# Row softmax in 3 whole-row buffers instead of 6 half-row buffers, and the last three stores moved to SyncE's queue

## The chip, the cores and the metric

The kernel runs on one core of a Trainium2 chip. The metric is the device time of one execution in microseconds (us). Three executions of the kernel before took 2497.65, 2497.72 and 2498.47 us; their median is 2497.72 us. The core has compute engines that run their own instruction streams; this kernel uses VectorE (DVE), ScalarE (ACT) and SyncE (SP, which here only issues transfers). Transfers between the core's memory (SBUF, 128 partitions) and the chip's main memory are issued from SP's queue and from ACT's queue, and 16 DMA engines carry them out.

## The reference

The kernel computes a softmax with temperature over the last axis of a float32 tensor of 16 x 256 x 32768. The temperature is 1.0.

```python
def reference(logits, temperature):
    scaled = logits / temperature
    scaled = scaled - scaled.max(axis=-1, keepdims=True)
    exp_scaled = np.exp(scaled)
    return (exp_scaled / exp_scaled.sum(axis=-1, keepdims=True)).astype(np.float32)
```

The tensor has 4096 rows of 32768 elements, 536.87 MB. It is read once and written once, so 1073.74 MB have to pass the DMA engines.

## The kernel before

**Tiles.** Each row is cut into two halves of 16384 elements, and each half takes one partition, so a tile is 128 partitions (64 rows) by 16384 elements (64 KB per partition, 8.39 MB). There are G = 64 tiles. A tile has C = 2 chunks of `_CW` = 8192 elements (32 KB per partition, 4.19 MB). SBUF holds `_BUFS` = 6 chunk buffers, three tiles' worth; chunk i lives in buffer i % 6 and its result is written in place.

**Loads and stores.** `load(i)` (lines 103 to 118) runs on SP's queue. It first waits until the buffer's earlier store has landed (line 106), then issues one DMA of 4.19 MB (line 112); in the first and the last tile each chunk is loaded as two pieces of `_EDGE` = 4096 elements (2.1 MB). `store(i)` (lines 120 to 133) runs on ACT's queue: it waits until DVE has scaled the chunk and issues one DMA (line 128), or two in the last tile.

**Compute of one tile** (lines 137 to 230). For each chunk DVE waits for its load and takes the negated maximum (line 156); ACT replaces the chunk by exp(x - max) and accumulates the sum (line 170). When ACT has finished the tile's last chunk, DVE swaps maxima and sums between the two partitions of one row (line 183) and takes the row's maximum (line 187), ACT forms the correction factors (line 194), DVE the corrected sum (line 200) and its reciprocal (line 212). Then DVE scales each chunk in place (line 221). In the last tile all this is done in four pieces of 4096 instead of two of 8192.

**Order.** Every engine's order is written out by hand; nothing is reordered. Six chunk loads are issued first. Then, tile by tile, comes the compute, and after it for each of the tile's chunks its store and the load of the chunk that takes its buffer, six chunks on. SP therefore issues loads alone, in order, each when its buffer's store has landed; ACT issues a tile's stores between its own work on that tile and on the next. The waits are semaphore waits of the issuing engine, so everything behind a wait on that engine is held up too.

```python
    for i in range(_BUFS):
        load(i)
    for g in range(G):
        compute(g)
        for c in range(C):
            i = g * C + c
            store(i)
            j = i + _BUFS
            if j < n_chunks:
                load(j)
```

Of the kernel before, what the change touches and what calls it, by code (L numbers as in the profile page):

```python
# [6 lines left out]


_CW = 8192
_BUFS = 6  # L10
_EDGE = 4096


class Stream:
# [40 lines left out]
@with_exitstack  # L55
def kernel(
    ctx: ExitStack,
    tc: tile.TileContext,
    logits: bass.AP,
    temperature: bass.AP,  # L60
    out: bass.AP,
):
    nc = tc.nc
    inv_t = 1.0 / float(temperature)
    P = nc.NUM_PARTITIONS
    fp32 = mybir.dt.float32
# [7 lines left out]
    C = W // _CW  # L74
    assert W * 2 == V and C * _CW == W and (N * 2) % P == 0
    x = xf.rearrange("n (h v) -> (n h) v", h=2)
    o = of.rearrange("n (h v) -> (n h) v", h=2)
    G = N * 2 // P
    n_chunks = G * C
    swap = [i ^ 1 for i in range(32)]  # L80

    ctx.enter_context(tc.tile_critical())  # L82
    X = nc.alloc_sbuf_tensor("xs", [P, _BUFS * _CW], fp32)
    KM = 2 * C
    T = [nc.alloc_sbuf_tensor(f"t{q}", [P, 4 * KM], fp32) for q in range(2)]
    E = [nc.alloc_sbuf_tensor(f"ee{q}", [P, 2 * KM], fp32) for q in range(2)]
    J = [nc.alloc_sbuf_tensor(f"junk{q}", [P, 2 * KM], fp32) for q in range(2)]
    R = [nc.alloc_sbuf_tensor(f"row{q}", [P, 4], fp32) for q in range(2)]

    sp = Stream(nc, nc.sync, "sp")  # L90
    dve = Stream(nc, nc.vector, "dve")
    act = Stream(nc, nc.scalar, "act")
    loads = [[Landing(nc, f"ld{b}{h}") for h in range(_CW // _EDGE)] for b in range(_BUFS)]
    stores = [Landing(nc, f"st{b}") for b in range(_BUFS)]
    scaled = {}
    landed = {}
    fine = {}
    freed = {b: [] for b in range(_BUFS)}

    def spans(total, step):  # L100
        return [(s, min(step, total - s)) for s in range(0, total, step)]

    def load(i):
        g, c = divmod(i, C)
        b = i % _BUFS
        sp.wait(*freed[b])
        pieces = spans(_CW, _EDGE if g in (0, G - 1) else _CW)
        rows = slice(g * P, (g + 1) * P)
        for k, (s, n) in enumerate(pieces):
            lane = loads[b][k]  # L110
            lane.add(
                nc.sync.dma_start(  # L112
                    out=X[:, b * _CW + s : b * _CW + s + n],
                    in_=x[rows, c * _CW + s : c * _CW + s + n],
                )
            )
        landed[i] = [lane.token() for lane in loads[b] if lane.count]
        fine[i] = len(pieces) > 1

    def store(i):  # L120

        g, c = divmod(i, C)
        b = i % _BUFS
        rows = slice(g * P, (g + 1) * P)
        for s, n in spans(_CW, _EDGE if g == G - 1 else _CW):
            act.wait(scaled[i, s])
            stores[b].add(
                nc.scalar.dma_start(
                    out=o[rows, c * _CW + s : c * _CW + s + n],
                    in_=X[:, b * _CW + s : b * _CW + s + n],  # L130
                )
            )
        freed[b] = [stores[b].token()]

    hist = {}

    def compute(g):
        step = _EDGE if g == G - 1 else _CW
        per = _CW // step
        K = C * per  # L140
        t, e, j_, r = T[g % 2], E[g % 2], J[g % 2], R[g % 2]
        tv = t[:, 0 : 4 * K].rearrange("p (a b k) -> p a b k", a=2, b=2)
        old = hist.get(g - 2)
        sums = []
        for c in range(C):
            i = g * C + c
            b = i % _BUFS
            for s, n in spans(_CW, step):
                k = c * per + s // step
                xs = X[:, b * _CW + s : b * _CW + s + n]  # L150
                piece = s // _EDGE
                dve.wait(*(landed[i][piece : piece + 1] if fine[i] and step == _EDGE else landed[i]))
                if old:
                    dve.wait(old["ee"], old["tr"])
                m = dve.done(
                    nc.vector.tensor_reduce(  # L156
                        out=t[:, k : k + 1], in_=xs, axis=mybir.AxisListType.X, op=A.max, negate=True
                    )
                )
                if inv_t != 1.0:  # L160
                    dve.wait(m)
                    m = dve.done(
                        nc.vector.tensor_scalar_mul(
                            out=t[:, k : k + 1], in0=t[:, k : k + 1], scalar1=inv_t
                        )
                    )
                act.wait(m)
                sums.append(
                    act.done(
                        nc.scalar.activation(  # L170
                            out=xs,
                            in_=xs,
                            func=Exp,
                            bias=t[:, k : k + 1],
                            scale=inv_t,
                            accum_out=t[:, K + k : K + k + 1],
                        )
                    )
                )
# [31 lines left out]
        dve.wait(tr)  # L211
        rc = dve.done(nc.vector.reciprocal(out=r[:, 2:3], in_=r[:, 1:2]))  # L212
        dve.wait(rc)
        for c in range(C):
            i = g * C + c
            b = i % _BUFS
            for s, n in spans(_CW, step):
                k = c * per + s // step
                xs = X[:, b * _CW + s : b * _CW + s + n]
                scaled[i, s] = dve.done(  # L220
                    nc.vector.tensor_scalar(  # L221
                        out=xs,
                        in0=xs,
                        scalar1=e[:, k : k + 1],
                        scalar2=r[:, 2:3],
                        op0=A.mult,
                        op1=A.mult,
                    )
                )
        hist[g] = {"ee": ee, "tr": tr}  # L230

    for i in range(_BUFS):
        load(i)
    for g in range(G):
        compute(g)
        for c in range(C):
            i = g * C + c
# [40 lines left out]
```

## Time and profile before

| what | value |
|---|---|
| time of the profiled execution | 2497.72 us |
| its span | 2495.9 us |
| median of three executions | 2497.72 us |
| moved by DMA | 1073.84 MB, mean 430 GB/s over the span |
| DVE busy | 1723.7 us (69%), 644 instructions |
| ACT busy | 944.5 us (38%), 325 instructions |
| store DMAs (ACT's queue) | 126 of 4096 KB and 4 of 2048 KB |
| load DMAs (SP's queue) | 124 of 4096 KB and 8 of 2048 KB |

The span is the stretch that the profile covers; 1.8 us of the time lie around it. Busy time is time in which an engine executes; the DMA rate is given by the profile for 40 equal slices of the span and, when asked, for any stretch. A packet is what one DMA engine moves in one go: here one partition's contiguous piece, 32 KB of a whole chunk and 16 KB of an edge piece, besides a 4-byte one per DMA and engine that counts up the semaphore.

### The profile page before, as it was taken

The numbers are of one execution on the slowest core, as the hardware profiler recorded it, in microseconds if no ns is written. First come the engines' busy times: TensorE is split into PE (matmuls) and PEld (weight loads), VectorE is DVE, ScalarE is ACT, GpSimd is POOL, SyncE is SP. The second block draws the span as 40 slices with busy tenths as digits, with TensorE's granted clock in tenths as the row PEclk, the third lists the DMA queues.
The fourth block names the chain that finished last, engine by engine and source line by source line (L and its number), as shares of the span: only waits on it lengthen the run. The fifth ranks groups of instructions, "written<-read, shape, count | busy, mean of one in ns | idle before, by whom it ended". The sixth has DMA issues, their size and how long they took to land.

```text
span 2495.9 us, 1288 instructions
## 1 busy us (share of the span) xinstructions
DVE 1723.7 (69%) x644; ACT 944.5 (38%) x325; POOL 0.2 (0%) x4
## 2 busy tenths in 40 slices
DVE  6777766767667676676766767767667676676763
ACT  3344334343343433434334333343333433434332
POOL 0000000000000000000000000000000000000000
DMA  9999999999999999999999999999999999999997
GB/s 412 432 433 435 430 436 430 436 430 436 432 434 435 431 435 430 436 431 434 435 431 436 429 437 430 436 432 433 435 430 435 431 436 432 434 434 431 435 433 337
DMA packets 37738, 1073.84 MB, mean 430 GB/s; under 512 B 4192, under 2 KB 4192, under 8 KB 4192
## 3 DMA queue, kind: packets, MB, share of 16 engines
q1 hardware_dynamic: 19008, 536.88, 49.9%
q10 hardware_dynamic: 18720, 536.88, 49.8%
q14 instruction: 10, 0.08, 0.0%
HBM read 536.87 MB, written 536.87 MB: 430 GB/s over the span
## 4 chain that ended last, share of the span: by engine, by line
DMA 62%; another core or an unknown queue 15%; DVE 15%; ACT 7%; SPq 0%; issue 0%; DVEq 0%
DMA out_dram<-xs 38%; DMA xs<-in_logits_dram 23%; DVE t L156 9%; ACT xs L170 7%; DVE xs L221 5%; SPq L112 0%; ACT ee L194 0%; DVE row L212 0%; DVE row L187 0%; DVE t L183 0%; DVE junk L200 0%; DVE row L200 0%; SPq L273 0%; DVEq L31 0%
## 5 line engine op out<-in xcount | busy, mean ns | idle before, releaser
L170 ACT ACTIVATE xs<-xs,t 128x8192 f32<-128x8192 f32 (+1 forms) x130 | 912.1, 7016 | 1498.5 <-DVE t L156 1498.5
L156 DVE TENSOR_REDUCE t<-xs 128x1 f32<-128x8192 f32 (+1 forms) x130 | 1111.1, 8551 | 263.8 <-DMA xs<-in_logits_dram 263.8
L221 DVE TENSOR_SCALAR xs<-xs,ee,row 128x8192 f32<-128x8192 f32 (+1 forms) x130 | 576.6, 4478 | 2.3
L183 DVE LOAD_MASK_SELECT t<-t x64 | 0.9, 14 | 463.1 <-ACT xs L170 463.1
L194 ACT ACTIVATE ee<-t,row 128x4 f32<-128x4 f32 x64 | 19.0, 297 | 27.0 <-DVE row L187 27.0
L200 DVE CUSTOM_DVE_ANT_1 junk<-ee,t 128x4 f32<-128x4 f32 x64 | 10.4, 163 | 23.3 <-ACT ee L194 23.3
L170 ACT ACTIVATION_READ_ACCUMULATOR xs<-xs,t 128x1 f32 x130 | 24.2, 186 | 0.0
L212 DVE RECIPROCAL row<-row 128x1 f32<-128x1 f32 x64 | 10.5, 164 | 2.2
L187 DVE TENSOR_REDUCE row<-t 128x1 f32<-128x4 f32 x64 | 10.1, 157 | 2.2
L183 DVE STREAM_SHUFFLE t<-t 128x4 f32<-128x4 f32 x64 | 9.9, 155 | 0.0
L200 DVE DVE_READ_ACCUMULATOR2_ANT row<- 128x1 f32 x64 | 5.3, 82 | 0.0
L170 ACT ACT_TABLE_LOAD x1 | 1.3, 1283 | 0.9 <-SPq L82 0.9
L259 POOL MEMSET const-bfloat16-1.0<- 128x1 bf16 x1 | 0.1, 101 | 0.0
L259 POOL MEMSET const-uint8-127<- 128x1 uint8 x1 | 0.1, 101 | 0.0
L259 POOL MEMSET const-float32-0.0<- 128x1 f32 x1 | 0.1, 98 | 0.2 <-issue 0.2
L259 POOL MEMSET const-float32-1.0<- 128x1 f32 x1 | 0.1, 98 | 0.0
## 6 DMA issues: line engine op xcount, KB each, us to landing
out_dram<-xs ACTq DMA_DIRECT2D x126, 4096.0 KB, 49.4
xs<-in_logits_dram SPq DMA_DIRECT2D x124, 4096.0 KB, 26.6
xs<-in_logits_dram SPq DMA_DIRECT2D x8, 2048.0 KB, 21.2
out_dram<-xs ACTq DMA_DIRECT2D x4, 2048.0 KB, 10.2
```

The source lines that it names most:

```text
L156: nc.vector.tensor_reduce(out=t[:, k : k + 1], in_=xs, axis=mybir.AxisListType.X, op=A.max, negate=True)
L170: nc.scalar.activation(out=xs, in_=xs, func=Exp, bias=t[:, k : k + 1], scale=inv_t, accum_out=t[:, K + k : K + k + 1],)
L183: nc.vector.stream_shuffle(out=t[:, 2 * K : 4 * K], in_=t[:, 0 : 2 * K], mask=swap)
L187: nc.vector.tensor_reduce(out=r[:, 0:1], in_=tv[:, :, 0, :], axis=mybir.AxisListType.XY, op=A.min)
L194: nc.scalar.activation(out=ev, in_=tv[:, :, 0, :], func=Exp, bias=r[:, 0:1], scale=-1.0)
L200: nc.vector.tensor_tensor_reduce(out=j_[:, 0 : 2 * K].rearrange("p (a k) -> p a k", a=2), in0=ev, in1=tv[:, :, 1, :], scale=1.0, scalar=0. ...
L212: rc = dve.done(nc.vector.reciprocal(out=r[:, 2:3], in_=r[:, 1:2]))
L221: nc.vector.tensor_scalar(out=xs, in0=xs, scalar1=e[:, k : k + 1], scalar2=r[:, 2:3], op0=A.mult, op1=A.mult,)
L259: nc = _bacc.Bacc("TRN2", target_bir_lowering=False, num_devices=1)
```

## The change

The chunk disappears as the unit of transfer and of buffering. `_BUFS` becomes 3 buffers of a whole tile (64 KB per partition, the same SBUF bytes in all). A load is one DMA of 8.39 MB, still four pieces of 4096 elements in the first and the last tile; it waits for the landing of the store of the whole tile that was in the buffer. A store is one DMA of 8.39 MB, four pieces in the last tile, issued when the whole tile is scaled. DVE and ACT work through a tile in three cuts of 6144, 6144 and 4096 elements instead of two of 8192; the last tile keeps its four pieces of 4096. A cut waits for the DMAs that cover it. The stores of the last `_LATE` = 3 tiles (61, 62 and 63) are issued on SP's queue instead of ACT's; in SP's program they come after the last load, since the load of tile 63 belongs to the loop's step of tile 60.

```diff
-_CW = 8192
-_BUFS = 6
+_BUFS = 3
+_CUTS = (0, 6144, 12288, 16384)
 _EDGE = 4096
+_LATE = 3
...
-    X = nc.alloc_sbuf_tensor("xs", [P, _BUFS * _CW], fp32)
-    KM = 2 * C
+    X = nc.alloc_sbuf_tensor("xs", [P, _BUFS * W], fp32)
+    KM = W // _EDGE
...
+    def cuts(g):
+        if g == G - 1:
+            return spans(W, _EDGE)
+        return [(a, z - a) for a, z in zip(_CUTS, _CUTS[1:])]
+
+    def load(g):
+        b = g % _BUFS
+        if b in freed:
+            sp.wait(freed[b])
+        for k, (s, n) in enumerate(spans(W, _EDGE if g in (0, G - 1) else W)):
+            loads[b][k].add(
                 nc.sync.dma_start(
...
+                    out=X[:, b * W + s : b * W + s + n],
+                    in_=x[g * P : (g + 1) * P, s : s + n],
+                )
+            )
+            landed.setdefault(g, []).append((s + n, loads[b][k].token()))
+
+    def store(g):
+
+        b = g % _BUFS
+        q = sp if g >= G - _LATE else act
+        for s, n in spans(W, _EDGE if g == G - 1 else W):
+            q.wait(scaled[g, s + n])
             stores[b].add(
...
+                q.engine.dma_start(
+                    out=o[g * P : (g + 1) * P, s : s + n],
+                    in_=X[:, b * W + s : b * W + s + n],
+                )
+            )
+        freed[b] = stores[b].token()
...
-        for c in range(C):
-            i = g * C + c
-            b = i % _BUFS
-            for s, n in spans(_CW, step):
...
+        for k, (s, n) in enumerate(cuts(g)):
+            xs = X[:, b * W + s : b * W + s + n]
+            first = 0
+            for z, token in landed[g]:
+                if first < s + n:
+                    dve.wait(token)
+                first = z
...
-    for i in range(_BUFS):
-        load(i)
+    for g in range(_BUFS):
+        load(g)
     for g in range(G):
         compute(g)
-        for c in range(C):
-            i = g * C + c
-            store(i)
-            j = i + _BUFS
-            if j < n_chunks:
-                load(j)
+        store(g)
+        if g + _BUFS < G:
+            load(g + _BUFS)
     sp.wait(*[s.token() for s in stores])
```

More of the change, by code (lines that the diff above doesn't have):

```diff
@@ L73 @@
     W = V // 2
-    C = W // _CW
-    assert W * 2 == V and C * _CW == W and (N * 2) % P == 0
+    assert W * 2 == V and _CUTS[-1] == W and (N * 2) % P == 0
     x = xf.rearrange("n (h v) -> (n h) v", h=2)
@@ L78 @@
     G = N * 2 // P
-    n_chunks = G * C
     swap = [i ^ 1 for i in range(32)]
     ctx.enter_context(tc.tile_critical())
-    X = nc.alloc_sbuf_tensor("xs", [P, _BUFS * _CW], fp32)
-    KM = 2 * C
+    X = nc.alloc_sbuf_tensor("xs", [P, _BUFS * W], fp32)
+    KM = W // _EDGE
     T = [nc.alloc_sbuf_tensor(f"t{q}", [P, 4 * KM], fp32) for q in range(2)]
@@ L92 @@
     act = Stream(nc, nc.scalar, "act")
-    loads = [[Landing(nc, f"ld{b}{h}") for h in range(_CW // _EDGE)] for b in range(_BUFS)]
+    loads = [[Landing(nc, f"ld{b}{h}") for h in range(KM)] for b in range(_BUFS)]
     stores = [Landing(nc, f"st{b}") for b in range(_BUFS)]
@@ L96 @@
     landed = {}
-    fine = {}
-    freed = {b: [] for b in range(_BUFS)}
+    freed = {}
+    hist = {}
     def spans(total, step):
         return [(s, min(step, total - s)) for s in range(0, total, step)]
-    def load(i):
-        g, c = divmod(i, C)
-        b = i % _BUFS
[L106 to L111, printed above, removed]
+    def cuts(g):
+        if g == G - 1:
+            return spans(W, _EDGE)
+        return [(a, z - a) for a, z in zip(_CUTS, _CUTS[1:])]
@@ L112, in load @@
+    def load(g):
[4 more added lines that the diff above has]
+            loads[b][k].add(
                 nc.sync.dma_start(
-                    out=X[:, b * _CW + s : b * _CW + s + n],
-                    in_=x[rows, c * _CW + s : c * _CW + s + n],
-                )
-            )
-        landed[i] = [lane.token() for lane in loads[b] if lane.count]
-        fine[i] = len(pieces) > 1
@@ L120, in store @@
[L120 to L126, printed above, removed]
+                    out=X[:, b * W + s : b * W + s + n],
+                    in_=x[g * P : (g + 1) * P, s : s + n],
+                )
+            )
+            landed.setdefault(g, []).append((s + n, loads[b][k].token()))
[4 more added lines that the diff above has]
+            q.wait(scaled[g, s + n])
@@ L127, in store @@
             stores[b].add(
-                nc.scalar.dma_start(
-                    out=o[rows, c * _CW + s : c * _CW + s + n],
-                    in_=X[:, b * _CW + s : b * _CW + s + n],
-                )
-            )
-        freed[b] = [stores[b].token()]
-    hist = {}
+                q.engine.dma_start(
+                    out=o[g * P : (g + 1) * P, s : s + n],
+                    in_=X[:, b * W + s : b * W + s + n],
+                )
+            )
+        freed[b] = stores[b].token()
@@ L137, in compute @@
     def compute(g):
-        step = _EDGE if g == G - 1 else _CW
-        per = _CW // step
-        K = C * per
+        b = g % _BUFS
+        K = len(cuts(g))
         t, e, j_, r = T[g % 2], E[g % 2], J[g % 2], R[g % 2]
@@ L144, in compute @@
         sums = []
-        for c in range(C):
-            i = g * C + c
-            b = i % _BUFS
-            for s, n in spans(_CW, step):
[L149 to L154, printed above, removed]
+        for k, (s, n) in enumerate(cuts(g)):
[5 more added lines that the diff above has]
+                first = z
+            if old:
+                dve.wait(old["ee"], old["tr"])
+            m = dve.done(
+                nc.vector.tensor_reduce(
+                    out=t[:, k : k + 1], in_=xs, axis=mybir.AxisListType.X, op=A.max, negate=True
+                )
+            )
+            if inv_t != 1.0:
+                dve.wait(m)
@@ L155, in compute @@
                 m = dve.done(
-                    nc.vector.tensor_reduce(
-                        out=t[:, k : k + 1], in_=xs, axis=mybir.AxisListType.X, op=A.max, negate=True
-                    )
-                )
[L160 to L177, printed above, removed]
+                    nc.vector.tensor_scalar_mul(
+                        out=t[:, k : k + 1], in0=t[:, k : k + 1], scalar1=inv_t
+                    )
+                )
@@ L178, in compute @@
+            act.wait(m)
+            sums.append(
+                act.done(
+                    nc.scalar.activation(
+                        out=xs,
+                        in_=xs,
+                        func=Exp,
+                        bias=t[:, k : k + 1],
+                        scale=inv_t,
+                        accum_out=t[:, K + k : K + k + 1],
                     )
                 )
+            )
         dve.wait(sums[-1])
@@ L213, in compute @@
         dve.wait(rc)
-        for c in range(C):
-            i = g * C + c
[L216 to L228, printed above, removed]
+        for k, (s, n) in enumerate(cuts(g)):
+            xs = X[:, b * W + s : b * W + s + n]
+            scaled[g, s + n] = dve.done(
+                nc.vector.tensor_scalar(
+                    out=xs,
+                    in0=xs,
+                    scalar1=e[:, k : k + 1],
+                    scalar2=r[:, 2:3],
+                    op0=A.mult,
+                    op1=A.mult,
                 )
+            )
         hist[g] = {"ee": ee, "tr": tr}
-    for i in range(_BUFS):
-        load(i)
+    for g in range(_BUFS):
+        load(g)
     for g in range(G):
         compute(g)
-        for c in range(C):
-            i = g * C + c
-            store(i)
-            j = i + _BUFS
-            if j < n_chunks:
-                load(j)
+        store(g)
+        if g + _BUFS < G:
+            load(g + _BUFS)
     sp.wait(*[s.token() for s in stores])
```

## The prediction

> **What bounds the kernel now.** I read the page's slices first, then the queues, SP's waits, stretches of the span, and the end in order of time. The page's slices and queues:
>
> ```profile
> DVE  6777766767667676676766767767667676676763
> DMA  9999999999999999999999999999999999999997
> GB/s 412 432 433 435 430 436 430 436 430 436 432 434 435 431 435 430 436 431 434 435 431 436 429 437 430 436 432 433 435 430 435 431 436 432 434 434 431 435 433 337
> ...
> q1 hardware_dynamic: 19008, 536.88, 49.9%
> q10 hardware_dynamic: 18720, 536.88, 49.8%
> ```
>
> The DMA engines are busy in every slice; only the first (412) and the last (337 GB/s) fall short. Loads (q1) and stores (q10) share them half and half. SP's waits say the same: a load waits for the store that frees its buffer.
>
> ```profile
> SPq L112 <- DMA out_dram<-xs: 2365.3, 122, 63.8
> ```
>
> So there are two places to gain: the rate of the packets, and the ends. In steady work a tile takes one period of transfers. From 600 to 1900 us 563.08 MB pass, 433.1 GB/s, which is 38.73 us per tile of 16.78 MB. Compute is shorter: in the time order the DVE starts a tile at 49.09 and the next at 83.68 us, 34.6 us, so DVE waits for data once the start is over.
>
> The end, in stretches of the span (length; busy DVE, ACT, POOL; clock; DMA share; GB/s):
>
> ```profile
> 2440.00:2462.00 22.00, 4.56 (x2) 5.67 (x4) 0.00 (x0) 1.00 1.02 437
> 2462.00:2471.00 9.00, 4.72 (x6) 4.10 (x3) 0.00 (x0) 1.00 0.09 36
> 2471.00:2476.00 5.00, 4.93 (x6) 0.00 (x0) 0.00 (x0) 1.00 0.37 157
> 2476.00:2480.00 4.00, 4.00 (x3) 0.00 (x0) 0.00 (x0) 1.00 0.93 393
> ```
>
> and the instructions behind it, in order of time:
>
> ```profile
> 2446.90 4.42 DVE L156 TENSOR_REDUCE t<-xs 128x1 f32<-128x4096 f32 x1 [8.87 <-DMA xs<-in_logits_dram]
> ...
> 2461.86 4.42 DVE L156 TENSOR_REDUCE t<-xs 128x1 f32<-128x4096 f32 x1 [10.54 <-DMA xs<-in_logits_dram]
> 2466.31 3.71 ACT L170 ACTIVATE xs<-xs,t 128x4096 f32<-128x4096 f32 x1 [11.15 <-DVE t L156]
> ...
> 2471.28 9.38 DVE L221 TENSOR_SCALAR xs<-xs,ee,row 128x4096 f32<-128x4096 f32 x4
> 2473.73 7.31 ACTq L128 DMA_DIRECT2D out_dram<-xs  x4
> ```
>
> The last load's pieces come in beside the stores of tile 62; when the last has landed (2461.9) nothing is left to move until tile 63 is reduced, exponentiated and scaled (2473.7), and then its whole 8.39 MB go out. The packet records of the trace put the slowest DMA engine's last semaphore packet before this gap at 2467.5 and its next packet at 2474.6: 7.0 us idle. (The other engines are up to 4.7 us ahead of it and idle longer; they don't set the end.)
>
> **The change, part by part.** The sum is against the profiled execution, 2497.72 us with a span of 2495.9, equal to the median; a measurement can tell about 0.2%, 5 us, from no change.
>
> *Larger packets.* The packet records show the price of a packet without overlap. At the start loads run alone: the pieces of 2 MB (8 packets of 16 KB per engine and a semaphore packet) complete at 12.19, 17.05 and 21.91 on the first engine, 4.86 us apart; the 4 MB loads that follow complete at 31.60 and 41.31, 9.70 us apart. Two pieces cost 9.72 to 9.73, so one merge of two DMAs saves about 0.03 us; successive starts on one engine (607 ns for 16 KB, 1209.5 for 32 KB) give 4.5 ns per packet saved, 0.036 us for 8 packets, and with the semaphore packet (9 ns) 0.04. I take 0.04. Merged are the loads of tiles 1 to 62 and the stores of tiles 0 to 62, 125 merges: **-5.0 us**. No row shows a 64 KB packet. Bounds: if the chip moves it as two of 32 KB the gain is 0; if the whole difference of the packets' own durations (2 x 611 - 1213 = 9 ns) counted, 125 x 8 x 9 ns = 9.0 us. I take the cadence, since the durations overlap each other.
>
> The Trainium skill ("DMA: Bandwidth & Descriptors", Why small descriptors are slow) gives a fixed cost of some 3 cycles per packet; at the 850 MHz that the page names for the fabric I estimate 3.5 ns, which would make 3.5 us of the 5.0 and the time 1.5 us longer. No run shows the cycles; my 4.5 ns stands.
>
> *Whole-tile buffers and three cuts.* Compute per tile: three reduces (6144 lies halfway between the rows of 4416 and 8682 ns: 6.55, 6.55, 4.42, 17.6 with their gaps); ACT takes 5.5, 5.5 and 3.8 with its accumulator read, starts the second cut at 13.2 and ends the third at 22.5; the small steps take 1.1 (39.05 to 40.17 in tile 0); scaling 9.0 for two pieces and 9.4 for four, so 9.2. Sum 32.8 against 34.6 us. DVE waits either way, so this saves nothing by itself; it pays for the coarser buffers. One buffer's lap: load landed to DVE start 0.4 (2461.5 to 2461.86), compute 32.8, issue to first packet 0.9 (2473.73 to 2474.57), store S, store landed to SP's issue 0.4 (68.30 to 68.69), issue to first packet 1.0 (0.94 to 1.95), load L. With both rings always busy S and L each take one period, 38.64: 35.5 + 77.3 = 112.8 us, against three periods, 115.9. There are 3.1 us to spare, and a ring that runs dry for a moment leaves the other at full rate (loads alone ran at 437 GB/s from 23.1 to 44.7). So **0 us**. The whole-row waits hold nothing else: behind ACT's store wait stand the exponentials of the next tile, whose reduces come on DVE only after that scaling; behind SP's wait stand only later loads.
>
> *Start.* The same 25 MB are requested first, in 6 DMAs instead of 8. The first store could be issued at 44.75 before; now the whole tile is scaled at about 13.3 + 32.8 = 46, with loads still in the ring until about 60 us. **0 us**.
>
> *Last three stores on SP.* SP issues six more DMAs (0.33 to 0.46 us each), off the path; ACT issues six fewer. They are held behind SP's wait for store 60 and behind load 63, and its ring. Count from load 63's first packet: load 63 has the engines alone, 4 x 4.87 = 19.5; store 61 follows, 19.3 (two 4 MB DMAs alone, 9.69 each, less the merge), then store 62: 58.2 us of transfers without a gap. Beside them DVE and ACT do tile 62 (0.4 + 32.8), tile 63's four reduces (17.8), its last exponential (3.9), the small steps (1.1) and the first scaling (2.4), with 0.9 to the first packet: 59.3. Gap 1.1; if load 62 was through before store 60 had landed there is instead one gap of 0.4 + 1.0 = 1.4 ahead of load 63, and compute has that head start. After that the scalings (2.4 each) outrun the pieces (4.9 each). So 7.0 us of idle becomes at most 1.4: **-5.6 us**. Bounds: 0 left, -7.0; or all of it stays, 0.
>
> A rule against this: the same page (Rules for kernel authors) says to issue a DMA early and wait late. By it the late store 61 loses; if the 19.5 us it waits behind load 63 reached the end, the time would be 2506. The rows speak the other way: the last load's final two pieces landed some 15 us apart beside stores (2446.9, 2461.86) where alone they need 4.9.
>
> *Sum:* 2497.72 - 5.0 - 5.6 = **2487 us** (-0.4%). One more term is open on both sides: the slowest engine lags by 4.75 us at the end because 10 packets of 8 KB on q14 (instructions) fell on it and a few others in the span; the five on it cost about 0.85 us each, 0.31 of their own and 0.54 by which they held up a packet. If packets of twice the size are held up twice as long the lag grows by 5 x 0.54 = 2.7 us; with other engines hit it shrinks by some such amount. Own range 2480 to 2492.
>
> **The rivals.**
>
> *The buffers run dry (slower).* The first store, issued at 44.75 beside running loads, saw its first packet only at 49.66: 4.9 us, because the engines had taken on load packets ahead. With packets twice as long this may grow. If such a wait counted as dead time in the lap, it decides from 3.1 us on: once per lap (4.9 - 1.0 = 3.9) gives 0.8/3 per tile, 16 us over 61 tiles, 2503; twice, 4.7/3, 96 us, 2583. Against it: in that wait the other ring moves data, so what one transfer loses the other gains.
>
> *Packets gain nothing.* A 64 KB piece is moved as two packets: 2492. For it: no row has such a packet; against it: 16 and 32 KB went as one each.
>
> *The end stays idle.* Tile 63's compute ends 5.6 us later than I count, and the ring stays empty for as long as before: 2492.7. Against it: load 63 lands at 19.5, some 13 us before DVE turns to it, and the durations summed vary by less than 0.1 us between tiles.
>
> *64 KB packets are slower,* by coarse turns between reading and writing. At 1% of 38.64 us per tile it is +24 us, 2511. Nothing from 16 to 32 KB hints at it.
>
> **How the numbers follow.** Forecast 0.62; buffers dry 0.14 (a third of it under 2506); packets nothing 0.09; end idle 0.07; slow packets 0.08. Faster takes the forecast, most of "packets nothing" and a share of "end idle": 0.70; same 0.11; slower 0.19. The range goes from 2479 to 2505: up to the once-per-lap case; the severe cases are left out.
>
> **What would show it.** Right: 10,944 packets on q1 and 8,784 on q10 (144 per DMA); the mean DMA rate in the middle 434 GB/s or more; loads of 8192 KB landing within about 40 us; in the last 80 us a stretch of loads only, then stores only, with no stretch under 300 GB/s; DVE's reduces of tile 63 with hardly any wait for DMA. Wrong: a DMA share below 1 in the middle slices, DVE and both queues waiting together, a period per tile above 38.7, or a gap between tile 62's store and tile 63's.

## The result and the profile after

The changed kernel takes 2515.25 us in the median of four executions against 2498.09 us before. Three of them lie between 2511.5 and 2515.6 us; the fourth took 2674.1 us, far above the others, and the ratio leaves it out: 1.0065 with a 95% interval of 1.0049 to 1.0080. It became 17 us slower. The forecast was 2487 us with a range up to 2505, so both the sign and the range were wrong.

The profiled execution took 2511.52 us with a span of 2509.7. Its page shows the slices and the queues:

```profile
DMA  9999999999999999999999999999999999999999
GB/s 418 433 418 433 433 422 433 424 429 432 435 420 435 435 432 428 419 426 435 433 420 432 428 425 433 430 425 433 434 429 424 433 432 421 435 434 419 420 424 410
DMA packets 19739, 1073.84 MB, mean 428 GB/s; under 512 B 2192, under 2 KB 2192, under 8 KB 2192
...
q1 hardware_dynamic: 10944, 562.04, 52.2%
q10 hardware_dynamic: 8784, 511.71, 47.8%
```

The packets are what the prediction counted, 10,944 on q1 and 8,784 on q10, one of 64 KB per partition. The last slice rose from 337 to 410 GB/s: the end was repaired. But the slices between, which never left 429 to 437 before, now dip to 418 to 425 every second or third, while the DMA share still reads full. From 500 to 2390 us the stretch view (start:end, length, busy time of DVE, ACT and POOL, clock, DMA share, GB/s) gives 429 GB/s where it was 433; the kernel before stands first:

```profile
500.00:2390.00 1890.00, 1310.25 (x489) 719.92 (x245) 0.00 (x0) 1.00 1.00 433
500.00:2390.00 1890.00, 1314.14 (x580) 720.31 (x336) 0.00 (x0) 1.00 1.00 429
```

So the middle lost more than the end gained, and it lost it with hardly any idle time (1.9 us per engine, below).

The chain of waits (start, length, what; all in us) shows the new bound:

```profile
352.42 41.00 DMA out_dram<-xs
393.44 44.02 DMA xs<-in_logits_dram
437.46 0.02 issue
437.48 13.02 DVE t L151 x2
450.51 0.02 issue
450.53 9.21 ACT xs L165 x4
...
460.89 9.20 DVE xs L212 x3
470.10 0.02 issue
470.12 42.44 DMA out_dram<-xs
```

Store, load, compute and store of one buffer follow one another without a gap, and no transfer waits behind a long queue of others: 470.12 - 352.42 = 117.7 us for one lap of a buffer, a third of which is 39.2 us per tile. Before, the first store of a tile waited 26 to 29 us in its ring for its first packet. A ring is the list of packets that one of the two queues still has to move on one engine. The second view shows stretches of the span around one turn, the place where a store and a load are issued (at 1017.66 and 1018.57 us):

```profile
1000.00:1016.00 16.00, 10.58 (x10) 7.57 (x5) 0.00 (x0) 1.00 0.99 430
1016.00:1028.00 12.00, 8.63 (x3) 0.41 (x1) 0.00 (x0) 1.00 0.97 350
1028.00:1054.00 26.00, 20.18 (x11) 14.59 (x7) 0.00 (x0) 1.00 0.98 423
```

For 12 us the engines are 97% busy at 350 GB/s. The packet records say what they are busy with. They name no engine; the order by engine is worked out from where one packet ends and the next starts. Given are the start in us and, where it isn't 2.418 us, the length in brackets; S is a store's and L a load's packet, a star the semaphore packet:

```
engine a: L1013.78 S*1016.19 L1016.20 L*1018.61 S1018.62(2.60) S1021.22(2.63) L1023.84(4.34) S1028.18 L1030.59
engine b: L1013.46 S*1015.88 L1015.88 L*1018.30 S1018.63(2.48) S1021.11(2.82) L1023.93(4.31) S1028.23 L1030.65
```

Both rings run out within one packet of each other; the new DMAs arrive in empty rings; and the packets around the arrival are stretched, on engine a by 0.18, 0.21 and 1.9 us. The same holds over the run: at an issue in the middle the engine furthest ahead had, in the median, 0.5 us of loads or 0.1 us of stores left until its part of the transfer ahead had landed, where it had 4.6 and 34 us before. The slowest engine still had 3.1 and 1.9 us, so it is not the one to go by. Summed over the span and divided by 16 engines, with the stretch being what a packet took over the usual 0.611, 1.213 or 2.418 us, the profiled executions divide like this (us per engine; overlap is the time by which successive packets' records overlap and is subtracted; the ends are what lies outside the packets):

| kernel | packets at their usual length | stretch | idle | overlap | ends | span |
|---|---|---|---|---|---|---|
| before | 2484.7 | 2.2 | 12.2 | 6.6 | 3.4 | 2495.9 |
| after | 2476.7 | 31.2 | 1.9 | 3.7 | 3.6 | 2509.7 |

The 13.8 us between the spans are -8.0 on packets, +2.9 on overlap, -10.3 idle and **+29.0 of stretch**. The first two make the -5.1 that the prediction had as -5.0; the idle time is that of the end; the stretch was in no term of it. Half of it, 15.2 us, lies on packets that end 2 to 4 us after an issue.

### The profile page after: what moved, and what is told of

It reads as the page before. It is cut to its first block, busy times and chain, and to the rows that moved or that the text cites. A ratio compares the mean times of both kernels' runs of the same rounds, so it can differ in the third digit from the quotient of the medians.

```text
span 2509.7 us, 1412 instructions
## 1 busy us (share of the span) xinstructions
DVE 1739.8 (69%) x770; ACT 962.2 (38%) x451; POOL 0.2 (0%) x4
## 3 DMA queue, kind: packets, MB, share of 16 engines
q1 hardware_dynamic: 10944, 562.04, 52.2%
q10 hardware_dynamic: 8784, 511.71, 47.8%
## 4 chain that ended last, share of the span: by engine, by line
DMA 68%; DVE 22%; ACT 9%; issue 0%; SPq 0%; DVEq 0%
DMA xs<-in_logits_dram 34%; DMA out_dram<-xs 34%; DVE t L151 13%; DVE xs L212 9%; ACT xs L165 9%; ACT ee L189 0%; DVE row L207 0%; DVE row L182 0%; DVE t L178 0%; DVE junk L195 0%; DVE row L195 0%; SPq L113 0%; SPq L261 0%; DVEq L32 0%; SPq L81 0%
## 5 line engine op out<-in xcount | busy, mean ns | idle before, releaser
L165 ACT ACTIVATE xs<-xs,t 128x6144 f32<-128x6144 f32 (+1 forms) x193 | 929.7, 4817 | 1493.6 <-DVE t L151 1493.6
L151 DVE TENSOR_REDUCE t<-xs 128x1 f32<-128x6144 f32 (+1 forms) x193 | 1109.7, 5805 | 408.2 <-DMA xs<-in_logits_dram 408.2
L212 DVE TENSOR_SCALAR xs<-xs,ee,row 128x6144 f32<-128x6144 f32 (+1 forms) x193 | 588.5, 3106 | 2.3
L165 ACT ACTIVATION_READ_ACCUMULATOR xs<-xs,t 128x1 f32 x193 | 36.0, 186 | 0.0
L189 ACT ACTIVATE ee<-t,row 128x6 f32<-128x6 f32 x64 | 19.2, 300 | 27.3 <-DVE row L182 27.3
L195 DVE CUSTOM_DVE_ANT_1 junk<-ee,t 128x6 f32<-128x6 f32 x64 | 10.7, 167 | 23.5 <-ACT ee L189 23.5
L207 DVE RECIPROCAL row<-row 128x1 f32<-128x1 f32 x64 | 10.5, 164 | 2.2
L182 DVE TENSOR_REDUCE row<-t 128x1 f32<-128x6 f32 x64 | 10.2, 159 | 2.2
L178 DVE STREAM_SHUFFLE t<-t 128x6 f32<-128x6 f32 x64 | 10.1, 158 | 0.0
```

Source lines behind the costliest of these rows:

```text
L151: nc.vector.tensor_reduce(out=t[:, k : k + 1], in_=xs, axis=mybir.AxisListType.X, op=A.max, negate=True)
L165: nc.scalar.activation(out=xs, in_=xs, func=Exp, bias=t[:, k : k + 1], scale=inv_t, accum_out=t[:, K + k : K + k + 1],)
L182: nc.vector.tensor_reduce(out=r[:, 0:1], in_=tv[:, :, 0, :], axis=mybir.AxisListType.XY, op=A.min)
L189: nc.scalar.activation(out=ev, in_=tv[:, :, 0, :], func=Exp, bias=r[:, 0:1], scale=-1.0)
L195: nc.vector.tensor_tensor_reduce(out=j_[:, 0 : 2 * K].rearrange("p (a k) -> p a k", a=2), in0=ev, in1=tv[:, :, 1, :], scale=1.0, scalar=0. ...
L212: nc.vector.tensor_scalar(out=xs, in0=xs, scalar1=e[:, k : k + 1], scalar2=r[:, 2:3], op0=A.mult, op1=A.mult,)
```

## The experiments

Two theories stood at the start. Theory 1: the rings run out at each turn and that is what stretches packets. Theory 2: a 64 KB packet costs by itself. Each time is a median, with its ratio to the kernel before and the 95% interval.

**The end alone, in the kernel before (before_late).**

```diff
+_LATE = 3
...
+        q = sp if g >= G - _LATE else act
         for s, n in spans(_CW, _EDGE if g == G - 1 else _CW):
-            act.wait(scaled[i, s])
+            q.wait(scaled[i, s])
...
-                nc.scalar.dma_start(
+                q.engine.dma_start(
```

> The kernel before with one part of the change: the stores of tiles 61 to 63 are issued on SP's queue behind the last load; chunks, packets and the six buffers stay. My theory of the end: the 7.0 us in which the slowest DMA engine stood idle before tile 63's store shrink to about 1.4, so 2498.1 - 5.6 = 2492.5 us, with no stretched packets in the middle. Rival: holding stores 61 and 62 behind load 63 costs what it gains, 2498 us or more.

Measured: 2490.97 us, 0.9973 (0.9962 to 0.9984), 6.7 us faster. The stretches of the end that were 36 and 157 GB/s before:

```profile
2440.00:2462.00 22.00, 16.88 (x12) 9.92 (x7) 0.00 (x0) 1.00 1.00 430
2462.00:2471.00 9.00, 0.00 (x0) 0.00 (x0) 0.00 (x0) 1.00 0.97 415
2471.00:2476.00 5.00, 0.00 (x0) 0.00 (x0) 0.00 (x0) 1.00 1.02 436
2476.00:2480.00 4.00, 0.00 (x0) 0.00 (x0) 0.00 (x0) 1.00 0.99 422
2480.00:2489.00 9.00, 0.00 (x0) 0.00 (x0) 0.00 (x0) 1.00 0.42 178
```

Compute is over before 2462, and transfers run on to the end. The last stretch ends with the slowest engine alone, some 5 us behind the others. This part of the change does what was predicted, and it is faster than both kernels.

**The end taken back out of the change (after_late0).**

```diff
-_LATE = 3
+_LATE = 0
```

> The changed kernel with its last three tiles' stores back on ACT's queue; all else is the change. If the end is worth the same here as in the kernel before (6.7 us), 2515 + 6.7 = 2522 us; if the rings' state in the middle hides it, 2515 us.

Measured: 2521.81 us, 1.0097 (1.0082 to 1.0112), some 7 us above the change. The end is worth about the same in both kernels, so the middle of the change lost some 24 us.

**The packet's price (before_16k).**

```diff
-        pieces = spans(_CW, _EDGE if g in (0, G - 1) else _CW)
+        pieces = spans(_CW, _EDGE)
...
-        for s, n in spans(_CW, _EDGE if g == G - 1 else _CW):
-            act.wait(scaled[i, s])
+        for s, n in spans(_CW, _EDGE):
+            act.wait(scaled[i, s if g == G - 1 else 0])
```

> The kernel before with every chunk loaded and stored as two DMAs of 2.1 MB back to back (packets of 16 KB), the waits at the same places. The price of a packet by itself: 124 loads and 126 stores are cut once, 250 x 0.04 us = +10 us, 2507.7 us. If a packet cost nothing by itself, 2497.7; if the durations of the records counted in full (8 x 9 ns each), +18 us, 2515.7.

Measured: 2501.43 us, 1.0024 (1.0009 to 1.0039), only 3.5 us above the kernel before. The records part this: packets at their usual length 2502.7 (+18.0), overlap 14.1 (7.5 more), so +10.5 on packets as expected; and idle 5.2 instead of 12.2, a gain of 7.0 at the end that I had not expected. The next kernel asks where it came from.

**Equal packets at the end (before_eq).**

```diff
-        for s, n in spans(_CW, _EDGE if g == G - 1 else _CW):
-            act.wait(scaled[i, s])
+        for s, n in spans(_CW, _EDGE if g >= G - 2 else _CW):
+            act.wait(scaled[i, s if g == G - 1 else 0])
```

> The kernel before with one thing else: tile 62's stores, too, are issued as pieces of 4096 elements, so that the packets that run beside the last load are 16 KB on both rings. Nothing is moved between queues. If an engine takes turns by packet whatever its size, the last load gets a half instead of a third of the engines, lands earlier, and the idle stretch before tile 63's store shrinks by some 7 us, as in the kernel with 16 KB packets throughout: 2498 - 7 + 0.3 = 2491 us. If it shares by bytes, nothing changes: 2498 us.

Measured: 2491.16 us, 0.9973 (0.9963 to 0.9983). One tile's stores in smaller packets are worth as much as moving three tiles' stores to another queue. In the kernel before, the queues from 2440 to 2455 us show why (packets, MB, share of the 16 engines):

```profile
q10 hardware_dynamic: 145, 4.23, 65.5%
q1 hardware_dynamic: 148, 2.16, 33.7%
```

The rings take as many packets each, 145 and 148, but the stores' are 32 KB and the last load's 16 KB, so the load gets a third of the engines. The Trainium skill ("DMA: Bandwidth & Descriptors", Queues, rings and completion order) says that an engine goes round its queues packet by packet; the counts agree. With 16 KB on both sides the last load's final two pieces complete 9.7 us apart instead of some 15, the last at 2455.0 instead of 2461.5.

**The same moments of issue in 32 KB packets (after_32k).**

```diff
-        for k, (s, n) in enumerate(spans(W, _EDGE if g in (0, G - 1) else W)):
+        for k, (s, n) in enumerate(spans(W, _EDGE if g in (0, G - 1) else W // 2)):
...
-                if first < s + n:
+                if first < s + n or 0 < g < G - 1:
...
-        for s, n in spans(W, _EDGE if g == G - 1 else W):
-            q.wait(scaled[g, s + n])
+        for s, n in spans(W, _EDGE if g == G - 1 else W // 2):
+            q.wait(scaled[g, s + n if g == G - 1 else W])
```

> The changed kernel with each transfer of 8.39 MB issued as two DMAs of 4.19 MB back to back, with the waits left where they are (a load waits for the whole tile's store, compute for the whole tile, a store for the whole scaled tile). Packets are 32 KB as before, the moments of issue those of the changed kernel. Theory 1, both rings nearly run out at once: the packets that are stretched after each issue stay, some 25 to 31 us per engine in all, and the saving of 5 us on packets is lost: 2516 to 2521 us. Theory 2, the 64 KB packet itself is what gets stretched when reads and writes take turns: the stretch goes, 2495 us or less.

Measured: 2548.87 us in the median of the three executions that the ratio of 1.0236 (1.0170 to 1.0302) rests on (2543.5 to 2577.7; a fourth took 2594.4). The stretch stays (34.7 us in the profiled execution, the shortest), so it is not a matter of 64 KB packets alone; but 25.4 us of idle come on top, which neither theory had, and the time is above what theory 1 gave. In the change a single 64 KB packet of one ring lasts 2.4 us and bridges the 1.4 us from a landing to the next first packet; one of 32 KB lasts 1.2. That this is the reason is argued from the durations, not shown.

**A shorter lap (after_shortmax, after_slack15).**

```diff
-                    out=t[:, k : k + 1], in_=xs, axis=mybir.AxisListType.X, op=A.max, negate=True
+                    out=t[:, k : k + 1], in_=xs[:, 0:1024], axis=mybir.AxisListType.X, op=A.max, negate=True
```

> The changed kernel with the maximum of each cut taken over its first 1024 elements only (the rest of the reduce is left out), 64 KB packets as they are. ACT then sets the pace: a tile is ready some 5.5 us earlier (first reduce 1.2, exponentials 14.8, small steps 1.1, scaling 9.2: 26.3 against 32.8 with the same start), so a store is issued while its ring still has work. Theory 1 (both rings nearly empty at each turn): the stretched packets fall from about 31 us per engine to under 12, 2485 to 2500 us. Theory 2 (64 KB packets): nothing changes in the middle, 2510 to 2516 us.

Measured: 2526.55 us, 1.0097 (1.0069 to 1.0126). That is no faster than the change; the median is 11 us above it, but the executions spread from 2502.6 to 2534.2 and the two intervals overlap, so "slower" is not shown. The lap in the profiled execution (2528.31 us) shows where the time went: from a load's landing to the store's issue 26.7 us instead of 33.1, but a load now takes 48.3 us from issue to landing on the slowest engine and 37.9 on the first, where it was 42.1 and 39.1. One engine fell some four load packets behind the first and ate what was saved. At a load's issue the slowest engine had 9.7 us of loads left in the median, but the engine furthest ahead had none, and none of stores at a store's issue: the turns stayed where both rings end together, with 43.0 us of stretch. My expectation for theory 1 missed.

The second kernel leaves out the scaling as well:

```diff
-            xs = X[:, b * W + s : b * W + s + n]
-            scaled[g, s + n] = dve.done(
-                nc.vector.tensor_scalar(
-                    out=xs,
...
-                )
-            )
+            scaled[g, s + n] = rc
```

> The changed kernel with the maximum over 1024 elements of each cut and the scaling left out (a store is issued when the reciprocal is there): the lap is about 15 us shorter, where the shorter maximum alone took 5.5 off and made the kernel slower (2526.6 against 2515). Theory 1: with some 18 us to spare at least one ring keeps work at each turn, the stretch falls under 10 us per engine, 2480 to 2495 us. Rival: the spare time is eaten again by a slow engine that falls behind (as the landings of the shorter maximum spread over 8.5 us) and the turns stay where both rings end together: 2515 to 2530 us.

Measured: 2507.68 us, 1.0023 (0.9993 to 1.0054), executions from 2487 to 2519. The median fits neither theory. The profiled execution is one of the shorter ones, 2490.48 us: there a load is issued with 11 us of work left in its ring on the engine furthest ahead and waits 13.7 us for its first packet, a store waits 4.9; the stretch is 9.1 us. So with some 15 us taken out of the lap the rings can stay fed, and then the time lies in the range that the prediction's own sum gave (2480 to 2492); what the longer executions did is not recorded.

**Loads in halves (after_loadhalves, after_halves_eq).**

```diff
-_CUTS = (0, 6144, 12288, 16384)
+_CUTS = (0, 8192, 12288, 16384)
...
-        for k, (s, n) in enumerate(spans(W, _EDGE if g in (0, G - 1) else W)):
+        for k, (s, n) in enumerate(spans(W, _EDGE if g in (0, G - 1) else W // 2)):
```

> The changed kernel with each load issued as two DMAs of 4.19 MB with a semaphore each, and cuts of 8192, 4096 and 4096, the first of which waits for the first half only. Stores stay whole, in packets of 64 KB. From the landing of the second half a tile takes two reduces of 4.4, one exponential of 3.8, 1.1 and 9.2, 23 us instead of 32.8, so the lap has 13 us to spare instead of 3. Theory 1: hardly any stretched packets, and 62 merges of loads lost at 0.04: 2487 + 2.5 = 2489.5 us. Theory 2: half of the packets are still 64 KB, so about half of the loss stays, 2500 us.

Measured: 2649.80 us, 1.0622 (1.0585 to 1.0660), with 76.3 us of stretch and 91.2 us of idle. Neither theory fits. I had put 32 KB loads beside 64 KB stores, which by the turns seen above gives the loads a third of the engines whenever both run: from 1076 to 1100 us the loads moved 3.64 MB and the stores 6.68 MB. That this alone cost the 150 us is not shown. The second kernel changes two things at once; it makes the packets equal and stores each half as soon as that half is scaled:

```diff
-        for s, n in spans(W, _EDGE if g == G - 1 else W):
+        for s, n in spans(W, _EDGE if g == G - 1 else W // 2):
             q.wait(scaled[g, s + n])
```

> The kernel of the loads in halves again, but with each store also issued as two DMAs of 4.19 MB, each as soon as its half is scaled; all packets of the middle are 32 KB, so both rings get equal turns. A load still waits until the whole tile that was in its buffer has been stored. With 32 KB loads beside 64 KB stores this lap took 2650 us; my reading is that the loads then got a third of the engines. Theory 1 (equal turns and a lap with 13 us to spare keep the rings fed): under 10 us of stretched packets, the 5 us saved on packets lost, the end as in the change: 2491 to 2500 us. Rival, that handing over whole buffers costs whatever the lap: 2540 us or more, as with whole tiles in 32 KB packets.

Measured: 2492.00 us, 0.9976 (0.9966 to 0.9985), all executions within 1 us. Its slices:

```profile
GB/s 412 430 436 431 436 432 432 434 432 435 430 437 430 436 431 433 434 433 435 430 437 429 436 431 433 435 431 436 429 437 430 437 431 434 434 432 435 431 408 405
```

The dips are gone and the stretch is 3.8 us. When a tile's first half is loaded, the ring has 4.6 us of work left on the engine furthest ahead and 8.1 on the slowest, about what a load had in the kernel before (4.8 and 7.3). This kernel keeps the change's three buffers, handed over whole, its queues and its end; it gives up the large packets and starts compute and stores by halves. Against the same buffers and packets with whole-tile waits (2548.87) that is 57 us.

**One ring dried out on purpose (before_dry).**

```diff
         sp.wait(*freed[b])
+        if i >= _BUFS:
+            sp.wait(landed[i - 1])
```

> The kernel before, with one wait more: from the seventh chunk on, SP also waits for the landing of the load ahead before it issues the next one, so that the load ring is empty at each of 122 issues while the store ring keeps a backlog of about 20 us. Theory 1a, a DMA issued into an empty ring beside a running one stretches the packets in progress (about 1 us per engine at the first store of before): 2498 + 122 x 0.4 to 1.0 = 2547 to 2620 us, with stretched packets after each load's issue. Theory 1b, only a turn at which both rings run out together costs: 2495 to 2505 us and no stretch.

Measured: 2659.00 us, 1.0659 (1.0636 to 1.0681), above what either form of theory 1 gave. SP's waits show that the new one holds every load:

```profile
SPq L31 <- DMA xs<-in_logits_dram: 2542.0, 122, 71.1
SPq L31 <- DMA out_dram<-xs: 53.7, 2, 31.4
```

The stretch is 81.3 us and the idle time 88.8. The sum of the stretch lies where theory 1a put it (0.4 to 1.0 us for each of 122 issues), but it does not lie at the issues that theory 1a named. The store ring's backlog did not last: from 190 us on stores, too, are issued again and again into a ring that has run empty, and the engines wait as well. So the trace holds several kinds of turn, which can be told apart by what the engine furthest ahead had left in each ring:

- At 65 of the 122 loads, each issued into the emptied load ring, no store was issued within 8 us into a ring with less than 2 us left. Packets that ended in the 8 us after such a load were stretched by 0.04 us per engine on average, by 0.31 at most.
- At 16 stores the store ring was empty, the load ring had more than 6 us left, and no load was issued in the 4 us before or the 7 us after. In the 8 us after such a store the stretch was 0.9 to 1.5 us, 1.1 on average. The load ring had itself been empty until 5 to 7 us before; at the first store of the kernel before (44.75 us), where loads had run from the start without a break, it was 0.9 us.

So in six buffers, with 32 KB packets and no other part of the change, a store issued into an empty ring beside running loads stretches packets, and a load issued into an empty ring beside running stores does not. Theory 1a holds for the stores alone. Theory 1b fails too, since the load ring had not run out at that first store. How much of the 161 us between the kernels goes back to which turns is not shown.

**No compute at all (after_nocompute, nocompute_32k, nocompute_64k).**

```diff
-        sums = []
         for k, (s, n) in enumerate(cuts(g)):
-            xs = X[:, b * W + s : b * W + s + n]
...
+            scaled[g, s + n] = [token for _, token in landed[g]]
```

> The changed kernel with all compute left out: a store is issued when its tile's load has landed, the buffers, the DMAs and their queues are those of the change. The lap of a buffer loses the 32.8 us of compute, so a ring has tens of us of work left when the next DMA is issued on it. Theory 1 (rings that run out): hardly any stretched packet, base rate of the 64 KB packets, 2498 - 5 on packets - 7 at the end, less a few us because the first stores start earlier: 2478 to 2487 us. Theory 2 (64 KB packets, or whole tiles handed over, cost by themselves): 2505 us or more, with packets stretched by some 30 us per engine as before.

Measured: 2499.47 us, 1.0008 (0.9993 to 1.0023), executions from 2491 to 2509. The profiled one (2492.19 us) has 6.3 us of stretch and, where no packet is stretched, 38.64 us per tile, the predicted period. But the median is no better than the kernel before, although this kernel does nothing but move data, and it fits neither theory. So it was run again beside a twin that issues each 8.39 MB as two DMAs of 4.19 MB at the same moment:

```diff
-        for k, (s, n) in enumerate(spans(W, _EDGE if g in (0, G - 1) else W)):
+        for k, (s, n) in enumerate(spans(W, _EDGE if g in (0, G - 1) else W // 2)):
...
-        for s, n in spans(W, _EDGE if g == G - 1 else W):
-            q.wait(scaled[g, s + n])
+        for s, n in spans(W, _EDGE if g == G - 1 else W // 2):
+            q.wait(scaled[g, W])
```

> The changed kernel with all compute left out and each 8.39 MB transfer issued as two DMAs of 4.19 MB (32 KB packets) at the same moment, whole tiles handed over as before. If the 64 KB packet is what makes the executions of the kernel without compute differ (2491 to 2509 us), these repeat within 1 or 2 us, at about 2491 + 5 = 2496 us by the price of a packet, or lower than the 64 KB kernel's median of 2499. If whole-tile hand-over is the cause, they differ by 10 us or more too.

> The changed kernel with all compute left out, again, on the same chip as its 32 KB twin: a median near 2499 us and executions that differ by 10 us or more if the first look holds; in the profiled execution a period of 38.64 us per tile where no packet is stretched.

Measured: with 32 KB packets 2487.42 us, 0.9959 (0.9945 to 0.9973), all five executions between 2487.33 and 2487.49; with 64 KB packets 2499.65 us, 1.0001 (0.9986 to 1.0016), ten executions between 2484.62 and 2504.36. The queues of the 32 KB kernel, then its slices and those of the 64 KB one:

```profile
GB/s 413 430 434 435 430 435 435 430 437 432 430 437 432 430 437 432 430 438 431 431 438 431 431 437 431 432 437 431 433 435 431 435 435 430 436 433 430 436 429 410
...
q1 hardware_dynamic: 20160, 562.05, 52.4%
q10 hardware_dynamic: 17568, 511.71, 47.7%
```

```profile
GB/s 421 427 433 435 432 430 437 436 434 431 435 433 433 433 429 434 434 430 432 433 434 430 435 432 431 430 438 432 433 431 433 434 433 431 429 438 430 430 433 402
```

The slices of the two hardly differ, but that is one of the shorter executions of the 64 KB kernel (2491.08 us). It has 10.6 us of stretch, all on load packets and spread over the time between the issues, where the 32 KB kernel has 1.4. So theory 2 holds in part: without compute, transfers in packets of 64 KB took 12 us more in the median, where the price of a packet promised a gain of 5; only the shortest execution, 2484.6, shows some of that gain. One rival is left: at a store's issue the engine furthest ahead had only 1.4 to 3.4 us of stores left in the 64 KB kernel and at least 5.5 in its twin, and whether that ring ran empty in the longer executions is not recorded.

All profiled executions together (us per engine; "fed" means that at all issues of the middle, but for one store in two of these kernels, the engine furthest ahead had 1 us or more left in the ring, "empty" that it often had not):

| kernel | rings at a turn | stretch | idle | span |
|---|---|---|---|---|
| before, before_late, before_eq, before_16k | fed | 2.2 to 2.9 | 5.0 to 12.2 | 2489 to 2500 |
| nocompute_32k | fed | 1.4 | 2.4 | 2485.5 |
| after_halves_eq | fed | 3.8 | 4.8 | 2490.2 |
| after_nocompute, nocompute_64k, after_slack15 | fed, 64 KB | 6.3 to 10.6 | 2.3 to 7.7 | 2489 to 2490 |
| after, after_late0, after_shortmax | empty, 64 KB | 31.2 to 43.0 | 1.9 to 7.1 | 2510 to 2527 |
| after_32k | empty | 34.7 | 25.4 | 2541.7 |
| after_loadhalves, before_dry | empty | 76.3, 81.3 | 91.2, 88.8 | 2647, 2652 |

## Why the prediction was wrong, point by point

*What bounds the kernel before* was read rightly: rate of the packets and the end.

*The last three stores on SP, -5.6:* right. Measured alone -6.7, and some -7 within the change.

*Start, 0:* right; the first store went out at 45.78 us (46 predicted), and the first two slices read 418 and 433 against 412 and 432.

*Larger packets, -5.0:* the arithmetic was right where a packet keeps its usual length (-5.1 by the records of before and after), and 38.64 us per tile was seen. The step failed as a forecast of time: it extended the line from 16 and 32 KB to 64 KB, and packets of that size are stretched now and then even in rings that did not run empty (10.6 us in the profiled execution without compute); the pair without compute is 12 us apart in the median the other way. The prediction named both bounds as gains and kept a loss for a rival at +24 us, with a chance of 0.08.

*Whole-tile buffers and three cuts, "So 0 us":* this is the step that broke the forecast. It rested on "both rings always busy" and on 3.1 us to spare, the lap being summed as 112.8 of 115.9 us, and the runs showed rings that run out at most turns and 29.0 us of stretched packets. Means over 50 tiles of the changed kernel:

| term of the lap, us | predicted | measured |
|---|---|---|
| load's landing to the store's issue | 33.2 | 33.05 |
| store's issue to landing | 0.9 + 38.64 | 41.75 |
| landing to the load's issue | 0.4 | 0.36 |
| load's issue to landing | 1.0 + 38.64 | 42.05 |
| sum | 112.8 | 117.2 |

Compute and hand-over were right to 0.2 us. Each transfer was 2.2 to 2.4 us longer. Two things were missed. The first packet came 2.8 us (store) and 4.3 us (load) after the issue, not 0.9 and 1.0: those rows were of engines that stood idle, and here the other ring's packet was under way. And a transfer has landed when the slowest engine is done, some 3 us behind the first, a lag that I had put only at the end of the kernel. Together 4.6 us, less 0.2 on compute and hand-over, used up the 3.1 to spare and 1.3 more: 0.4 us per tile, 27 us over the run. The table tells where the time went and not what came first, since the measured transfers contain the stretch itself (29.0 us over 61 tiles are 1.4 us per lap). Nor is the lap the whole cause: taking 6.4 us of compute out of it made the kernel no faster, and its lap stayed near 118 us, because the engines do not wait, they run stretched packets. The second sentence that failed is "a ring that runs dry for a moment leaves the other at full rate". The kernel with the dried-out load ring bears it out for loads (0.04 us at 65 issues) and refutes it for stores (1.1 us at 16); in the change both rings ran out together. It had only the loads before any store to rest on; the row that spoke against it stood in the same trace: at 46 to 49 us, when the first store came into an empty ring, 32 packets took 1.3 to 2.0 us instead of 1.2, about 0.9 us per engine. I had read those 4.9 us to the first packet as harmless because data moved.

*The rivals.* "The buffers run dry" was the right one, with a chance of 0.14. Its price of 16 us for one wait per lap had the right sign but was too low, the measured loss of the middle being 24 us; and its mechanism, a wait that counts as dead time, was only half of it, since the engines were not idle. Its counter-argument, "what one transfer loses the other gains", is what the stretch refutes. Its threshold of 3.1 us was not tested by itself: with 6.4 us less compute the rings still ran empty.

*The rule against the change* ("issue early") was weighed rightly: the late issue gained.

What stays open is why a packet is stretched when a store arrives in an empty ring and not when a load does, and why packets of 64 KB are stretched now and then in a fed one. The records give the time and the place, not the reason.

## What to carry to other kernels

When a kernel is bound by two transfer rings, count what each ring has left at the moment of the next issue, on the engine that is furthest ahead, and look at the store ring first. With 0.5 us of loads and 0.1 us of stores left the saving per packet (0.04 us per merged DMA here) was lost many times over; with 4.6 and 34 us left, in the kernel before, hardly a packet was stretched (2.2 us in all). Here, handing data over in halves kept a backlog in both rings. Keep packets that run beside each other equal in size, since the rings took turns by packet and not by byte. Look at the end on its own; 7 us lay there for two different small edits, and both beat the large one.

## What the runs showed of the hardware that was not expected

- Busy DMA engines can be slow engines: 97% busy at 350 GB/s for 12 us around a turn. The busy share does not show it; the GB/s and the lengths of the packets do.
- A load issued into an empty ring beside running stores stretched nothing to speak of (0.04 us at 65 issues); a store issued into an empty ring beside running loads cost 1.1 us per engine (16 issues).
- Packets of 64 KB without compute: executions from 2484.6 to 2504.4 us, where the same transfers in 32 KB repeat within 0.2 us at 2487.4.
- In an emptied ring the large packets are the lesser evil: 2515 us against 2549 in 32 KB, with 1.9 us of idle against 25.4.
- Fewer DMAs did not mean less time: the Trainium skill ("SBUF — State Buffer", The DMA setup-cost knee) advises the largest single transfer, for a fixed cost of some 2 us each. Back to back in a fed ring that cost was not there, 9.70 us for 4.19 MB and 4.86 us for half of it, and the kernel with the largest transfers lost to its twin with halves, 2499.65 against 2487.42.
